# Two gates on weight splits: none beside a power on GpSimd, and few while ScalarE and VectorE have a backlog

## The chip, the core and the metric

The program runs on one core of a Trainium2 chip. The metric is the time of one execution in microseconds (us) of device time. Three runs of the kernel before gave 1283.79, 1284.68 and 1285.19 us, a median of 1284.68 us. A profiled execution of its own is the source of all rows below. TensorE is written PE in the rows (PEld is its weight load), VectorE DVE, ScalarE ACT, GpSimd POOL and SyncE SP.

## What is computed

Two blocks of two layers each on 256 tokens of width 1024, all in float32. The first block has a short convolution mixer, a SwiGLU feed-forward layer, a windowed attention with sinks (16 query heads, 4 key heads), and a second SwiGLU layer:

```
x = x + short_conv_mixer(rmsnorm(x)) ; x = x + swiglu_ffn(rmsnorm(x))
x = x + swa_sink_attention(rmsnorm(x)) ; x = x + swiglu_ffn(rmsnorm(x))
```

The second block has a mixed attention (8 windowed heads with rotary positions, 8 neighbourhood heads with a position bias), a squared-ReLU layer, a bidirectional Mamba-2 mixer (eight groups of four heads), and a squared-ReLU layer, each followed by a layer norm:

```
x = layer_norm(ALPHA * x + mix(x)) ; x = layer_norm(ALPHA * x + squared_relu_mlp(x))
```

In the first attention the queries and keys are normalised per head, and a softmax over 128 or 256 keys and one sink gives the weights. In the Mamba-2 mixer each group's result y is normalised: its squares are summed, the sum plus a small number is raised to the power -0.5, and y is multiplied by that.

## The kernel before

**Weights.** Every weight matrix is cut into units of 128 x 2048 numbers (201 units). A unit comes by one 1 MB transfer into one of three raw buffers. Since the fast matmul reads rounded numbers, a unit is split into two tiles, hi and lo, in four parts of 128 x 512: ScalarE casts hi<-raw, VectorE subtracts lo<-raw,hi (`split_part`). Each product of two such pairs takes three matmuls (hi hi, hi lo, lo hi). So there are 804 casts and 804 subtractions, 769 of them on VectorE and 35 on GpSimd, which `beside` puts there in the Mamba-2 mixer. Five buffers of split units exist.

**Order.** The order of all instructions is fixed while the program is written, by a planner: `Clock` keeps a modelled time for each engine, for each written tile and for PSUM banks, and each recorded instruction moves it. A main thread writes the big matmuls one after the other, and between groups of three it calls `step`, which first calls `Units.fill` and then `Side.run`. `fill` writes splits ahead of their use; `Side.run` advances side tasks (softmax of a pair of heads, transposes, norms), each of which names the tiles that it needs and is taken when the planner thinks that they are ready. Every engine then works through its own instructions strictly in that order.

**How far ahead.** `fill` counts the parts that are split and not yet in use. With fewer than 8 of them (two units) a split is "late" and is written at once, one in each step, whatever the engines have to do. With 8 or more it is written only if the planner sees both ScalarE and VectorE idle. `get` writes at once what a matmul needs and nobody has split.

**Places that matter here.** (1) `attn1`, the first attention: `tok_mm` for the values ends with a copy of the bank into the tile `vt` on ScalarE (`nc.scalar.copy(out=vt[:, t, :], in_=ps[:, 0:256])`); the side task `heads_out`, which multiplies softmax weights by `vt`, asks for the softmax weights and for the task that marks `vt` as written, not for the time at which it is written. The exponentials of the softmax stand on ScalarE too. (2) `group_out` in `ssm`, the Mamba-2 mixer: squares on ScalarE, `rstd` (one VectorE addition to a tile sm, then a power of 128 x 2 numbers on GpSimd), a scaling on ScalarE, four transposes on PE, and a second split of the result. (3) `w_half`, the output product of the mixer: `row_mm` reads four units of 12 matmuls for each half of the tokens, so it uses up a unit in the time of 12 matmuls of 512 columns. All operations are recorded by one helper, so nearly every row has the line L162; the tiles tell them apart (g and sm are pools of work tiles, bank is a PSUM bank, xt the transposed activations).

Of the kernel before, what the change touches and what calls it, by code (L numbers as in the profile page):

```python
# [29 lines left out]
def _free(ap):  # L30
    n = 1
    for s in ap.shape[1:]:
        n *= s
    return n


class Clock:
# [11 lines left out]
    def __init__(self):  # L49
        self.at = dict.fromkeys(self.LAG, 0.0)  # L50
        self.cold_until = 0.0
        self.port = 0.0
        self.written = {}
        self.read = {}
        self.floor = {}
        self.bank = {}
# [26 lines left out]
    def op(self, eng, cost, outs, ins, port=False):  # L83
        t = self.at[eng]
        if port:
            t = max(t, self.port)
        for a in ins:
            t = max(t, self.ready(a, eng))
        for a in outs:
            t = max(t, self.floor.get(a.tensor.name, 0.0))  # L90
        banks = [self.bank.setdefault(a.tensor.name, {}) for a in ins + outs if a.tensor.space == PSUM]
        for b in banks:
            t = max([t] + [end + 130.0 for e, end in b.items() if e != eng])
        if eng == "pe":
            if t - self.at[eng] > self.IDLE:
                self.cold_until = t + self.WARM
            if t < self.cold_until:
                cost *= 2.0
        end = t + cost
        self.at[eng] = end  # L100
        for b in banks:
            b[eng] = end
        if port:
            self.port = end
        for a in ins:
            n = a.tensor.name
            self.read[n] = max(self.read.get(n, 0.0), end)
        for a in outs:
            w = self.written.setdefault(a.tensor.name, {})
            for b in self.blocks(a):  # L110
                w[b] = (end, eng)


class Engine:
# [7 lines left out]
    def cost(self, op, out, ins, kw):  # L122
        n = _free(out)
        src = max(n, max((_free(a) for a in ins if a.tensor.name != out.tensor.name), default=0))
        if self.name == "pe":
            if op == "transpose":
                return 107.0
            if out.shape[0] == 64:
                return 2.5 + max(n, 128) / 1.2
            return 2.5 + (n / 2.4 if ins[0].dtype == F32R and n >= 256 else max(n, 128) / 0.6)  # L130
        from_psum = any(a.tensor.space == PSUM for a in ins)
        if self.name == "act":
            ptr = sum(not isinstance(kw.get(k, 0.0), (int, float)) for k in ("scale", "bias"))
            return (50 if from_psum else 95) + 0.833 * n + 93 * ptr + (90 if "accum_out" in kw else 0)
        if self.name == "dve":
            if op == "memset":
                return 60 + 0.26 * n
            if op == "reciprocal":
                return 65 + 6.3 * n
            n += 62 * any(hasattr(kw.get(k), "tensor") for k in ("scalar", "scalar1", "scalar2", "accum_out"))  # L140
            fast = op in ("tensor_copy", "tensor_scalar") and not from_psum and out.tensor.space != PSUM
            return 65 + (0.52 if fast else 1.04) * (src if op in ("tensor_reduce", "bn_stats") else n)
        return 300 + 165.0 * n if kw["op"] == ALU.pow else 125 + 2.15 * n

    def __getattr__(self, op):
        f = getattr(self.engine, op)

        def emit(*args, **kw):
            aps = [a for a in args if hasattr(a, "tensor")]
            outs = [kw[k] for k in ("out", "accum_out") if k in kw]  # L150
            ins = [v for k, v in kw.items() if k not in ("out", "accum_out") and hasattr(v, "tensor")]
            if not outs:
                outs, aps = aps[:1], aps[1:]
            ins = [a for a in aps + ins if a.tensor.name in self.clock.written]
            if self.name == "dma":
                n = outs[0].shape[0] * _free(outs[0]) * 4
                self.clock.op("dma", 60 + n / 359.0, [o for o in outs if o.tensor.space == bass.MemoryType.SB], ins)
            else:
                n_sb = sum(a.tensor.space != PSUM and _free(a) > 1 for a in ins)
                port = self.name == "pool" or self.name == "dve" and n_sb > 1  # L160
                self.clock.op(self.name, self.cost(op, outs[0], ins, kw), outs, ins, port)
            return f(*args, **kw)  # L162

        return emit
# [160 lines left out]
class Units:  # L325
# [2 lines left out]

    PARTS = 4
    AHEAD = 8  # L330

    def __init__(self, nc, clock, raw_pool, n_raw, w_pool, n_w):
        self.nc = nc
# [53 lines left out]
    def fill(self):  # L387

        at = self.clock.at
        while self.room():  # L390
            now = at["pe"] + 100.0
            late = self.parts - self.used * self.PARTS < self.AHEAD
            if self.clock.ready(self.raws[self.parts // self.PARTS], "act") > now:
                break
            if not late and (at["dve"] > now or at["act"] > now):
                break
            self.split_part()
            if late:
                break
# [1506 lines left out]
```

## Time and profile before

| what | value |
|---|---|
| median of three runs | 1284.68 us |
| profiled execution: its own time | 1285.68 us |
| span from first to last instruction | 1283.8 us |
| PE busy | 1255.0 us (98%) |
| VectorE, ScalarE, GpSimd busy | 951.9, 703.6, 82.4 us |
| mean granted TensorE clock | 0.993 |

A busy share is a share of the whole span; a matmul's end is modelled, so a busy PE can still have small gaps. The granted clock is 1.00 at 2.4 GHz and 0.50 at 1.2 GHz.

### The profile page before, as it was taken

The numbers are of one execution on the slowest core, as the hardware profiler recorded it, in microseconds if no ns is written. First come the engines' busy times: TensorE is split into PE (matmuls) and PEld (weight loads), VectorE is DVE, ScalarE is ACT, GpSimd is POOL, SyncE is SP. The second block draws the span as 40 slices with busy tenths as digits, with TensorE's granted clock in tenths as the row PEclk, the third lists the DMA queues.
The fourth block names the chain that finished last, engine by engine and source line by source line (L and its number), as shares of the span: only waits on it lengthen the run. The fifth ranks groups of instructions, "written<-read, shape, count | busy, mean of one in ns | idle before, by whom it ended". The sixth has DMA issues, their size and how long they took to land.

```text
span 1283.8 us, 18806 instructions
## 1 busy us (share of the span) xinstructions
PE 1255.0 (98%) x7092; PEld 1078.1 (84%) x7092; DVE 951.9 (74%) x1858; ACT 703.6 (55%) x1571; POOL 82.4 (6%) x69
## 2 busy tenths in 40 slices
PE   7999999999899999999999999999999989999997
PEld 6998888888678888888888888889989868888885
DVE  6776766677787666669788575689989878775665
ACT  5544555556665555556646464536777855554540
POOL 1000000002100000000000000002314130000000
PEclk9999999999899999999999999999999989999999
DMA  7753655546236555554447555454415144565530
GB/s 264 258 208 142 209 186 196 191 170 215 98 131 218 179 193 197 181 195 146 181 164 255 194 197 198 169 191 144 155 69 197 66 164 135 198 234 187 189 140 33
DMA packets 39436, 225.92 MB, mean 176 GB/s; under 512 B 5552, under 2 KB 7088, under 8 KB 13744
## 3 DMA queue, kind: packets, MB, share of 16 engines
q1 hardware_dynamic: 39344, 224.71, 49.5%
q8 instruction: 56, 0.92, 0.3%
q14 instruction: 36, 0.29, 0.1%
HBM read 223.51 MB, written 1.05 MB: 175 GB/s over the span
## 4 chain that ended last, share of the span: by engine, by line
PE 92%; DVE 4%; ACT 2%; DMA 1%; POOL 0%; issue 0%; SPq 0%; POOLq 0%; DVEq 0%; ACTq 0%
PE bank L162 92%; DVE g L162 3%; ACT g L162 1%; DVE lo L162 1%; DMA raw<-in_w_conv_in_dram 1%; POOL sm L162 0%; ACT hi L162 0%; DVE x L162 0%; SPq L162 0%; DVE sm L162 0%; ACT xt L162 0%; POOLq L1902 0%; DVE xt L162 0%; DVEq L1902 0%; ACT sm L162 0%
## 5 line engine op out<-in xcount | busy, mean ns | idle before, releaser
L162 PE MATMUL bank<-xt,hi 128*128 128x256 f32 (+1 forms) x1984 | 529.6, 340 | 0.2
L162 DVE TENSOR_TENSOR lo<-raw,hi 128x512 fp32r<-128x512 f32 x769 | 486.9, 689 | 45.7 <-ACT hi L162 38.4
L162 ACT CAST hi<-raw 128x512 fp32r<-128x512 f32 x804 | 444.6, 621 | 54.7 <-issue 31.8
L162 PE MATMUL bank<-xt,lo 128*128 128x256 f32 x1472 | 414.9, 282 | 0.0
L162 PEld LDWEIGHTS bank<-xt,hi 128*128 128x128 f32 x1984 | 342.2, 191 | 48.9 <-issue 1.6
L162 PE MATMUL bank<-hi,g 128*128 128x512 f32 x1184 | 381.0, 394 | 0.4 <-ACT g L162 0.2
L162 PEld LDWEIGHTS bank<-xt,lo 128*128 128x128 f32 x1472 | 280.0, 190 | 1.2
L162 PEld LDWEIGHTS bank<-hi,g 128*128 128x128 f32 x1184 | 223.0, 188 | 50.8 <-issue 2.3
L162 PE MATMUL bank<-lo,g 128*128 128x512 f32 x592 | 231.7, 391 | 1.5 <-DVE lo L162 1.5
L162 DVE TENSOR_TENSOR g<-bank,g 128x256 f32<-128x256 f32 (+5 forms) x210 | 95.1, 463 | 159.0 <-ACT g L162 153.0
L162 PE MATMUL bank<-hi,xt 128*128 128x512 f32 (+1 forms) x608 | 188.6, 380 | 0.0
L162 ACT COPY g<-bank 128x256 f32<-128x256 f32 (+2 forms) x163 | 66.6, 412 | 216.8 <-PE bank L162 216.6
L162 PEld LDWEIGHTS bank<-lo,g 128*128 128x128 f32 x592 | 111.7, 189 | 24.0 <-DVE lo L162 2.4
L162 PEld LDWEIGHTS bank<-hi,xt 128*128 128x128 f32 x608 | 111.4, 188 | 20.3 <-issue 0.3
L162 PE MATMUL bank<-lo,xt 128*128 128x512 f32 (+1 forms) x304 | 113.6, 374 | 0.0
L162 POOL TENSOR_TENSOR sm<-sm,nhalf 128x1 f32<-128x1 f32 (+3 forms) x30 | 33.4, 1113 | 1103.6 <-DVE sm L162 826.6
L162 DVE TENSOR_TENSOR g<-g,g 128x512 fp32r<-128x512 f32 (+4 forms) x99 | 63.6, 653 | 32.4 <-ACT g L162 31.6
L162 ACT CAST g<-g 128x512 fp32r<-128x512 f32 (+1 forms) x48 | 29.2, 611 | 79.5 <-DVE g L162 79.5
L162 PEld LDWEIGHTS bank<-lo,xt 128*128 128x128 f32 x304 | 57.4, 189 | 9.2 <-DVE lo L162 0.4
L162 PE MATMUL bank<-ident,g 128*128 128x128 f32 (+1 forms) x328 | 51.3, 289 | 12.5 <-DVE g L162 8.3
L162 PEld LDWEIGHTS bank<-ident,g 128*128 128x128 f32 x328 | 41.8, 149 | 23.5 <-DVE g L162 9.3
L162 PE MATMUL bank<-g,g 128*128 128x64 f32 (+6 forms) x428 | 54.4, 332 | 4.3 <-ACT g L162 4.3
(83 smaller groups left out, 721.8 us busy)
## 6 DMA issues: line engine op xcount, KB each, us to landing
raw<-in_w_mlp_dram SPq DMA_DIRECT2D x64, 1024.0 KB, 4.9
raw<-in_w_gate_up_dram SPq DMA_DIRECT2D x44, 1024.0 KB, 4.9
raw<-in_w_in_s_dram SPq DMA_DIRECT2D x24, 1024.0 KB, 4.9
raw<-in_w_down_dram SPq DMA_DIRECT2D x22, 1024.0 KB, 4.9
raw<-in_w_conv_in_dram SPq DMA_DIRECT2D x11, 1024.0 KB, 5.7
raw<-in_w_in_dram SPq DMA_DIRECT2D x8, 1024.0 KB, 4.9
raw<-in_w_out_s_dram SPq DMA_DIRECT2D x8, 1024.0 KB, 4.9
raw<-in_w_conv_out_dram SPq DMA_DIRECT2D x4, 1024.0 KB, 5.0
```

What stands on the lines that cost most here:

```text
L162: return f(*args, **kw)
```

## The change

The planner remembers when the last power on GpSimd ends (any GpSimd instruction with at most 8 numbers a partition), and `fill` has two new gates. A split is late if fewer than 4 parts are ahead, or if fewer than 8 are ahead and neither VectorE nor ScalarE is modelled to be busy for more than 1200 ns beyond now. And with at least 4 parts ahead none is written while the last power ends later than what VectorE has been given.

```diff
+        self.power = 0.0
...
+        if eng == "pool" and _free(outs[0]) <= 8:
+            self.power = end
...
+    SHORT = 1200.0
...
-            late = self.parts - self.used * self.PARTS < self.AHEAD
+            ahead = self.parts - self.used * self.PARTS
+
+            late = ahead < self.PARTS or ahead < self.AHEAD and max(at["dve"], at["act"]) < now + self.SHORT
             if self.clock.ready(self.raws[self.parts // self.PARTS], "act") > now:
                 break
+
+            if ahead >= self.PARTS and self.clock.power > at["dve"]:
+                break
             if not late and (at["dve"] > now or at["act"] > now):
                 break
```

No instruction is added or removed: casts, subtractions and matmuls are as many as before, and 35 subtractions stay on GpSimd. What moves is the order, since a split that comes elsewhere moves the planner's clocks and with them the side tasks. Up to the first attention the orders are nearly alike; in both attentions and in the Mamba-2 mixer they differ in many places.

ScalarE in the first attention, from the exponentials of the second token half to the copy into `vt` (tile g_2838) of the first half. Before:

```order
L162 ACTIVATE g_3264<-bank 128x512
L162 ACTIVATE g_3212,sm<-g_3212,sm 128x256 x2
L162 ACTIVATE g_3213,sm<-g_3213,sm 128x256 x2
L162 ACTIVATE sm<-sm 128x4
L162 ACTIVATE g_3235,sm<-g_3235,sm 128x256 x2
L162 ACTIVATE g_3236,sm<-g_3236,sm 128x256 x2
L162 ACTIVATE sm<-sm 128x4
L162 CAST hi<-raw 128x512 x4
L162 COPY g_2838<-bank 128x256
```

Now (g_3172, g_3173, g_3188 and g_3189 are the same softmax tiles; their exponentials stand just ahead of this piece):

```order
L165 ACTIVATE sm<-sm 128x4
L165 CAST hi<-raw 128x512
L165 ACTIVATE g_3228<-bank 128x512
L165 CAST hi<-raw 128x512
L165 ACTIVATE g_3267<-bank 128x512
L165 CAST hi<-raw 128x512
L165 COPY g_3285<-bank 128x512
L165 CAST hi<-raw 128x512 x2
L165 COPY g_3309<-bank 128x512
L165 CAST hi<-raw 128x512
L165 COPY g_2838<-bank 128x256
```

The eight exponentials and four casts stood right before the copy; now the squares of two query chunks and the copies of the transposed softmax tiles (g_3285, g_3309) lie between, with one cast at the end. On PE the transposes of those softmax tiles stand among the 24 value matmuls of the first half, where they came after the multiplication by `vt` before.

VectorE at the start of `w_half`, around the addition (TENSOR_SCALAR sm<-sm) that feeds the power of group 6. Before (g_10364 and g_10198 are convolution results of group 7):

```order
L162 SCALAR_TENSOR_TENSOR g_10364<-bank,wc,g_10364 128x255 x4
L162 SCALAR_TENSOR_TENSOR g_10364<-bank,wc,g_10364 128x254 x4
L162 SCALAR_TENSOR_TENSOR g_10198<-g_10351,g_10198 128x512
L162 TENSOR_TENSOR lo<-raw,hi 128x512 x2
L162 TENSOR_SCALAR sm<-sm 128x2
L162 TENSOR_TENSOR lo<-raw,hi 128x512 x4
L162 SCALAR_TENSOR_TENSOR g_10364<-g_10436,g_10364 128x512
L162 TENSOR_TENSOR lo<-raw,hi 128x512 x3
L162 SCALAR_TENSOR_TENSOR g_10527<-bank,sm,g_10526 128x256 x2
```

Now (g_10363 and g_10231 are those results):

```order
L165 TENSOR_TENSOR lo<-raw,hi 128x512
L165 SCALAR_TENSOR_TENSOR g_10231<-g_10352,g_10231 128x512
L165 SCALAR_TENSOR_TENSOR g_10363<-bank,wc,g_10363 128x255 x4
L165 SCALAR_TENSOR_TENSOR g_10363<-bank,wc,g_10363 128x254 x4
L165 TENSOR_SCALAR sm<-sm 128x2
L165 TENSOR_TENSOR lo<-raw,hi 128x512 x3
L165 SCALAR_TENSOR_TENSOR g_10363<-g_10434,g_10363 128x512
L165 TENSOR_TENSOR lo<-raw,hi 128x512 x4
L165 SCALAR_TENSOR_TENSOR g_10502<-bank,sm,g_10501 128x256 x2
```

Behind the addition stand three subtractions, a gate product and four more subtractions, where there were four, the product and three. The two subtractions that stood just ahead of it are gone from there.

ScalarE at the same place, from the squares of group 6 to its scaling (g_10187 before, g_10196 now), which waits for the power. Before:

```order
L162 ACTIVATE g_10408,sm<-g_10187 128x256 x2
L162 CAST hi<-raw 128x512 x4
L162 ACTIVATE g_10436<-g_10364 128x512
L162 CAST hi<-raw 128x512 x3
L162 ACTIVATE g_10187<-g_10187,sm 128x256 x2
```

Now:

```order
L165 ACTIVATE g_10360,sm<-g_10196 128x256 x2
L165 CAST hi<-raw 128x512 x3
L165 ACTIVATE g_10434<-g_10363 128x512
L165 CAST hi<-raw 128x512
L165 ACTIVATE g_10196<-g_10196,sm 128x256 x2
L165 CAST hi<-raw 128x512 x3
```

Seven casts stood between the squares and the scaling; now there are four, and the next three come behind the scaling.

## Rows read from the trace of the kernel before

**Rows 1.** The page: busy time of the engines, share of the span, instructions

```profile
PE 1255.0 (98%) x7092; PEld 1078.1 (84%) x7092; DVE 951.9 (74%) x1858; ACT 703.6 (55%) x1571; POOL 82.4 (6%) x69
```

**Rows 2.** Waits of PE: who waited for whom: total us, times, longest us

```profile
PE bank L162 <- DVE g L162: 9.1, 3, 8.3
PE bank L162 <- ACT g L162: 8.5, 3, 4.3
PE bank L162 <- DVE lo L162: 1.5, 2, 1.3
```

**Rows 3.** Windows: length, then each engine's busy us (instructions), granted clock, DMA

```profile
331.90:336.50 4.60, 0.33 (x3) 0.13 (x2) 4.07 (x16) 4.55 (x16) 1.64 (x1) 0.76 0.00 0
336.50:341.20 4.70, 4.69 (x17) 3.08 (x18) 2.96 (x6) 1.92 (x4) 0.00 (x0) 0.50 0.30 82
...
1040.90:1049.20 8.30, 2.80 (x10) 1.34 (x8) 7.16 (x14) 2.76 (x7) 5.29 (x1) 0.91 0.69 255
1049.20:1054.50 5.30, 5.29 (x14) 4.19 (x15) 2.16 (x4) 1.20 (x3) 0.00 (x0) 0.50 0.53 195
```

**Rows 4.** Timeline of PE, first attention: start, length, what, idle before, releaser

```profile
331.95 0.28 PE L162 MATMUL bank<-hi,xt 128*128 128x256 f32 x1
336.51 1.98 PE L162 MATMUL bank<-g,g 128*64 128x512 f32 x4 [4.27 <-ACT g L162]
...
346.00 0.28 PE L162 MATMUL bank<-hi,xt 128*128 128x256 f32 x1
```

**Rows 5.** Timeline of ACT there: four casts, and both copies into vt

```profile
334.03 2.16 ACT L162 CAST hi<-raw 128x512 fp32r<-128x512 f32 x4
336.10 0.36 ACT L162 COPY g<-bank 128x256 f32<-128x256 f32 x1
...
346.51 0.34 ACT L162 COPY g<-bank 128x256 f32<-128x256 f32 x1
```

**Rows 6.** Timeline of PE around the start of w_half

```profile
1033.05 0.40 PE L162 MATMUL bank<-xt,hi 128*128 128x256 f32 x2
...
1033.41 0.40 PE L162 MATMUL bank<-hi,g 128*128 128x512 f32 x1
...
1040.69 0.61 PE L162 MATMUL bank<-hi,g 128*128 128x512 f32 x2
1042.63 0.50 PE L162 MATMUL bank<-lo,g 128*128 128x512 f32 x1 [1.32 <-DVE lo L162]
...
1049.21 1.30 PE L162 MATMUL bank<-ident,g 128*128 128x128 f32 x4 [3.98 <-ACT g L162]
```

**Rows 7.** Timeline of POOL: four of the eight powers of the Mamba-2 mixer

```profile
945.34 1.08 POOL L162 TENSOR_TENSOR sm<-sm,nhalf 128x2 f32<-128x2 f32 x1 [6.14 <-DVE sm L162]
...
1023.48 0.70 POOL L162 TENSOR_TENSOR sm<-sm,nhalf 128x2 f32<-128x2 f32 x1 [8.48 <-DVE sm L162]
...
1043.33 5.29 POOL L162 TENSOR_TENSOR sm<-sm,nhalf 128x2 f32<-128x2 f32 x1 [5.36 <-DVE sm L162]
1075.52 1.07 POOL L162 TENSOR_TENSOR sm<-sm,nhalf 128x2 f32<-128x2 f32 x1 [26.90 <-DVE sm L162]
```

**Rows 8.** Timeline of DVE around the power at 1043.33

```profile
1038.17 3.20 DVE L162 SCALAR_TENSOR_TENSOR g<-bank,wc,g 128x255 f32<-128x255 f32 x8
...
1043.17 2.49 DVE L162 TENSOR_TENSOR lo<-raw,hi 128x512 fp32r<-128x512 f32 x4
...
1046.17 1.89 DVE L162 TENSOR_TENSOR lo<-raw,hi 128x512 fp32r<-128x512 f32 x3
```

**Rows 9.** Timeline of DVE beside the powers at 945.34 and 1075.52

```profile
945.17 1.89 DVE L162 TENSOR_TENSOR lo<-raw,hi 128x512 fp32r<-128x512 f32 x3
...
1075.35 1.89 DVE L162 TENSOR_TENSOR lo<-raw,hi 128x512 fp32r<-128x512 f32 x3
```

**Rows 10.** Timeline of ACT at the start of w_half, and the scaling after the power

```profile
1033.62 1.02 ACT L162 ACTIVATE g<-bank,wc 128x256 f32<-128x256 f32 x2 [2.80 <-PE bank L162]
...
1048.65 0.91 ACT L162 ACTIVATE g<-g,sm 128x256 f32<-128x256 f32 x2 [5.06 <-POOL sm L162]
```

## The prediction

> **What bounds the kernel now.** I read the busy times first: TensorE is busy for 1255.0 us of a span of 1283.8 us [rows 1], so the kernel is its stream of matmuls, and only time that TensorE loses can be won. The waits of TensorE come next: 9.1, 8.5 and 1.5 us [rows 2]. One of these, 8.3 us, is the start of the program, which the change leaves as it is. What is left is 10.8 us, and two places hold nearly all of it; the windows and timelines show them.
>
> The first is in the first attention. The value matmuls of the first token half end at about 332.2, and TensorE then idles for 4.27 us until 336.51 [rows 4]. It waits for the copy of these values into `vt`, 0.36 us on ScalarE. That copy starts only at 336.10, behind the exponentials and four casts of 2.16 us together [rows 5]. After the pause the granted clock is 0.50, 1.2 GHz: from 336.50 to 341.20 TensorE is busy for 4.69 us at half speed [rows 3], which costs about 2.35 us more. Together 6.6 us.
>
> The second is in the Mamba-2 mixer, at the start of `w_half`. TensorE waits 1.32 us (1.5 with the small one after it [rows 2]) for a `lo` tile, and then 3.98 us for a scaling on ScalarE [rows 6]. The scaling had waited 5.06 us for a power [rows 10]. That power took 5.29 us, where others of its size took 0.70 to 1.08 [rows 7]. It ended 0.56 us after the last of a row of subtractions and products on VectorE that started at 1043.17 and ended at 1048.06 [rows 7, 8]. Then 5.29 us of matmuls ran at a clock of 0.50 [rows 3], which costs 2.65. Together 1.5 + 4.0 + 2.65 = 8.2 us (rounded).
>
> **The change part by part.** Nothing is added or removed on any engine, so busy time is the same, and what counts is where TensorE waits in the new order.
>
> *The copy into `vt`.* In the new order the eight exponentials stand well ahead, and right before the copy stand one softmax copy and one cast. On TensorE the transposes which that softmax copy reads are followed by 15 value matmuls of 256 columns. Three such matmuls start within 1033.41 - 1033.05 = 0.36 us [rows 6], so 15 take 1.8 us, and two ScalarE instructions of 0.5 to 0.6 us [rows 5] fit in. So the copy comes without a queue. `heads_out` is still placed right behind the value matmuls, so TensorE waits for the bare copy: the second copy started 0.51 us after the last value matmul had started and took 0.34 [rows 4, 5], 0.85 us, of which one matmul's 0.12 us is no wait. I take 0.8 us, and no lower clock, since the two drops of this trace stand behind pauses of 4 us. Saved: 6.6 - 0.8 = 5.8 us. Bounds: 0 if something of the old length is in front of it again, 6.6 if the copy is hidden.
>
> *The power.* I count from S, the first matmul of `w_half` (1033.41 before). Before, VectorE did the last eight convolution steps from S + 4.8 [rows 8], since group 6's result came late; in the new order the matmuls that give this result stand 48 matmuls of 256 columns ahead of S instead of 12, so that group's arithmetic on VectorE lies mostly ahead of S, and the convolution steps wait only for the ScalarE instruction that starts them, S + 0.2 to S + 1.2 [rows 10]. They take 3.2 us [rows 8]: S + 4.4. The addition follows, and the power starts at about S + 4.6. With 0.70 to 1.08 us [rows 7] it ends by S + 5.7, the scaling of 0.91 us [rows 10] by S + 6.7. Its transposes stand behind 33 matmuls; before, 32 of these started within 1040.69 - 1033.41 = 7.28 us [rows 6], so they come at S + 7.5. Slack 0.8 us: no wait.
>
> But the gate does not keep the splits away here. Three subtractions, a product and four more subtractions stand right behind the addition, because fewer than four parts are ahead in `w_half` and the power gate doesn't hold then. If the power is held as before, VectorE still runs dry sooner: only one cast is left before the scaling, so after five instructions of 0.62 us each (2.49 / 4 [rows 8]) VectorE has to wait, at S + 7.7. The power then ends 0.56 later at S + 8.3, the scaling at S + 9.2, and TensorE waits 1.7 us. How often is a power held? Three powers have three or more subtractions beside them: at 945.34 and 1075.52 they took 1.08 and 1.07 [rows 7, 9], at 1043.33 it took 5.29. One in three; I take the short one.
>
> The Trainium skill, "SBUF — State Buffer", section "Who interferes with whom", says that a VectorE instruction with two SBUF inputs and a GpSimd instruction that reads SBUF shut each other out, whoever starts first. The row at 1043.33 agrees, those at 945.34 and 1075.52 agree for the first subtraction only. By the rule taken to its end the new order would block this power as well, which is the first rival below.
>
> *The late `lo`.* TensorE waited because the convolution steps stood in front of the twelfth subtraction for `w_half`. Now the three subtractions behind the addition include the twelfth: S + 4.6 + 3 x 0.62 = S + 6.5, and it is read by the 34th matmul, after S + 7.5. So the 1.5 us go too, with 1.0 us to spare. Saved at this place: 8.2 us; between 3.9 (held power, and the low clock again: 8.2 - 1.7 - 2.65) and 8.2.
>
> *New waits.* The attentions and the eight groups are laid out anew, and the planner still doesn't see every wait: side tasks that ask for a task and not for a time, copies that land behind four exponentials of 0.5 us. The trace can't show them. Beside the two places TensorE lost 10.8 - 4.3 - 4.0 - 1.5 = 1.0 us in the whole kernel [rows 2]. The bounds for new ones are 0 and 6.6 us, one more of the kind of `vt`. I take 3: the two attentions and the groups were nearly free of waits before, and a new layout is more likely to have some.
>
> **Sum.** 5.8 + 8.2 - 3 = 11.0 us. The profiled execution took 1285.68 us (its span 1283.8 and 1.9 around it), so it would take 1274.7; it lies 1.0 us above the median of the runs, 1284.68, so the median would be 1273.7. I say 1274. The forecast's own range is 1270 to 1277.5: 14.0 us saved without new waits, about 7 with the full 6.6.
>
> **Rivals.**
>
> *The power is held again* (the change doesn't do what it says at the place that matters). For it: the three subtractions right behind the addition. Against it: two of three such powers were not held. The saving is 5.8 + 3.9 - 3 = 6.7 us: 1278. The same time results if the copy waits as before and the power is free (8.2 - 3 = 5.2: 1279.5).
>
> *The waits move.* Two new waits of the kind of `vt`, each 4.27 us and 2.35 us of low clock: 14.0 - 13.2 = 0.8 us saved, 1284, no change. For it: in the second half of the first attention the copies of `heads_out` now stand behind eight exponentials (4 us), where before four of them stood in front. Against it: 18 matmuls of 512 columns, 4.1 us by the rate above, cover most of that.
>
> *Splits come too late* (slower). Both gates let TensorE come closer to the split parts, four instead of eight ahead in a backlog. A subtraction that lands behind a convolution step then costs what it cost at 1042.63, about 1.5 us with its follower [rows 2], once for each of the 32 units of the Mamba-2 mixer at worst. Slower starts where such waits eat the 14.0 us and 2.6 more: 11 of them; with 16 it is 14.0 - 24 = -10, 1295 us. For it: when `w_half` starts, nine parts of its weights are split in the new order, eleven before. Against it: from the start to 290 us and from 400 to 575 the two orders are nearly alike, and nine parts are three quarters of what the first 36 matmuls use.
>
> **How the numbers follow.** Forecast (both waits gone): 0.50. Held power, or one of the two places only: 0.25. Moved waits, no change: 0.12. Late splits, slower: 0.13. Runs of this kernel can tell 0.2%, 2.6 us, from no change. So faster 0.75, the same 0.12, slower 0.13. The range of eight in ten starts at 1268, a little below all savings without a new wait (1270.7), and ends at 1285, so that it holds the no-change case; the late splits are left out above it.
>
> **What would show it.** Right: no idle of TensorE over 1 us behind the value matmuls of the first attention, no stretch at a clock of 0.50 between the start and the end, and the power of group 6 at about 1 us. The first rival: a power of 3 to 4 us beside subtractions, and TensorE waiting for ScalarE behind 33 matmuls of `w_half`. The second: new waits of PE for ACT g of 3 us or more in the attentions. The third: the total of PE waiting for DVE lo at 15 us or more. The forecast as a whole is wrong if busy time of TensorE at full clock changes by more than 2 us, since no instruction was added.

## The result, and the profile after

The changed kernel took 1299.07 us (median of four runs, 1298.61 to 1301.63), the kernel before 1284.24 (four runs, 1283.63 to 1285.19). The ratio is 1.0119, with a 95% interval of 1.0106 to 1.0132. It is slower by 15 us, where 1274 had been forecast. Its profiled execution took 1298.61 us with a span of 1296.8, 13.0 more than before. Rows of the changed kernel have the line L165 where those of before have L162.

The page of the changed kernel, busy time of the engines, is the counterpart of [rows 1]:

```profile
PE 1257.8 (97%) x7092; PEld 1081.8 (83%) x7092; DVE 943.1 (73%) x1858; ACT 704.1 (54%) x1571; POOL 75.5 (6%) x69
```

No instruction was added. PE's busy time grew by 2.8 us, which is matmuls at a lower clock (below); the other 10 of the 13 us are idle time of PE. The waits of PE after (who waited for whom, total us, times, longest us), against [rows 2]:

```profile
PE bank L165 <- DVE lo L165: 10.9, 10, 4.2
PE bank L165 <- DVE g L165: 9.5, 2, 9.2
PE bank L165 <- ACT hi L165: 7.2, 5, 2.5
PE bank L165 <- ACT g L165: 1.9, 3, 1.0
PE bank L165 <- POOL lo L165: 0.7, 2, 0.4
```

The wait for DVE g is still the start of the program, 0.9 us longer than before. The waits for ACT g, which the forecast wanted to remove, fell from 8.5 to 1.9 us. But PE now waits for the split weights themselves, hi and lo: 10.9 + 7.2 + 0.7 = 18.8 us in 17 waits, where there were 1.5 in two.

The longest of these waits is in the first attention. The timeline of PE there (start, length, what, idle before and its releaser):

```profile
315.78 0.39 PE L165 MATMUL bank<-hi,xt 128*128 128x512 f32 x1
316.37 0.50 PE L165 MATMUL bank<-hi,xt 128*128 128x512 f32 x1 [0.20 <-ACT hi L165]
321.08 0.65 PE L165 MATMUL bank<-lo,xt 128*128 128x512 f32 x1 [4.21 <-DVE lo L165]
```

The timeline of VectorE ahead of it shows what stood in front of that `lo`:

```profile
303.28 0.68 DVE L165 TENSOR_TENSOR lo<-raw,hi 128x512 fp32r<-128x512 f32 x1
305.50 0.69 DVE L165 TENSOR_TENSOR g<-bank,sm 128x512 f32<-128x512 f32 x1 [1.54 <-POOL sm L165]
...
309.82 0.69 DVE L165 TENSOR_TENSOR lo<-raw,hi 128x512 fp32r<-128x512 f32 x1 [1.28 <-ACT hi L165]
...
315.84 0.69 DVE L165 TENSOR_REDUCE sm<-g 128x8 f32<-128x512 f32 x1 [2.52 <-ACT g L165]
...
318.55 0.69 DVE L165 TENSOR_TENSOR g<-bank,sm 128x512 f32<-128x512 f32 x1 [0.63 <-POOL sm L165]
...
319.55 0.88 DVE L165 TENSOR_SCALAR g<-g,sm 128x128 f32<-128x128 f32 x4
320.34 3.09 DVE L165 TENSOR_TENSOR lo<-raw,hi 128x512 fp32r<-128x512 f32 x5
```

Between 303.28 and 320.34 VectorE wrote one part, though it idled five times (four of them, 1.54, 1.28, 2.52 and 0.63 us, are in these rows). Then five subtractions came at once, behind two rounds of softmax and a head norm. How many parts were written shows in the windows of VectorE, counting only its `lo` instructions (length, busy us and number, clock, DMA). Before:

```profile
280.00:300.00 20.00, 8.02 (x13) 1.00 0.55 190
300.00:320.00 20.00, 7.10 (x11) 1.00 0.57 206
```

After:

```profile
280.00:300.00 20.00, 6.12 (x10) 1.00 0.53 185
300.00:320.00 20.00, 3.35 (x5) 1.00 0.45 159
```

Five against eleven: in the same 20 us TensorE ate what had been split ahead and then stood still.

Behind the pauses the clock fell. The windows of the three stretches at half clock (compare [rows 3]; a stretch behind the last weight matmul, which both kernels have, is left out):

```profile
321.30:324.70 3.40, 3.40 (x16) 2.77 (x15) 2.13 (x4) 1.27 (x2) 0.00 (x0) 0.50 0.37 96
355.40:362.20 6.80, 5.33 (x22) 4.27 (x24) 4.18 (x10) 1.48 (x3) 0.00 (x0) 0.50 0.46 153
1041.50:1048.30 6.80, 6.64 (x31) 6.64 (x32) 5.19 (x10) 2.71 (x6) 0.00 (x0) 0.50 0.52 166
```

15.37 us of busy time at half speed cost 7.7 us, where the 4.69 + 5.29 us of before cost 5.0 [rows 3]. The difference, 2.7 us, is nearly all of the 2.8 us of busy time.

At the two places of the forecast the waits did shrink. The copy into `vt` is now bare; the row answers to [rows 4]:

```profile
337.98 0.28 PE L165 MATMUL bank<-hi,xt 128*128 128x256 f32 x1
338.78 1.08 PE L165 MATMUL bank<-g,g 128*64 128x512 f32 x4 [0.52 <-ACT g L165]
```

And at the start of `w_half` the power of group 6 was held again, but shorter, as the first rival had worked out. First POOL, then the subtractions of VectorE beside it, then PE (compare [rows 6, 7, 8]):

```profile
1060.25 3.48 POOL L165 TENSOR_TENSOR sm<-sm,nhalf 128x2 f32<-128x2 f32 x1 [0.26 <-DVE sm L165]
```

```profile
1060.08 1.89 DVE L165 TENSOR_TENSOR lo<-raw,hi 128x512 fp32r<-128x512 f32 x3
```

```profile
1062.91 0.39 PE L165 MATMUL bank<-hi,g 128*128 128x512 f32 x1
1064.33 0.94 PE L165 MATMUL bank<-ident,g 128*128 128x128 f32 x4 [1.03 <-ACT g L165]
```

The account: at the two places 4.27 - 0.52 + 2.35 = 6.1 us and 1.5 + 3.98 - 1.03 + 2.65 = 7.1 us came in. The split waits and the clock behind them took 18.8 + 7.7 = 26.5. That makes 13.3 us longer; the span says 13.0. By place the 26.5 us are 14.4 in the first attention (10.0 of waits, the rest clock), 1.7 in the second and 10.4 in the Mamba-2 mixer (7.1 of waits, 5.4 of them for casts, and clock). The close agreement is in part luck: the first attention lost 10.6 us (table below), where these terms give 14.4 - 6.1 = 8.3, and the stretch ahead of that attention was 1.3 us shorter in this execution than in that of before.

### The profile page after: what moved, and what is told of

It is laid out like the page before. It is cut to its first block, busy times and chain, and to the rows that moved or that the text cites. A ratio compares the mean times of both kernels' runs of the same rounds, so it can differ in the third digit from the quotient of the medians.

```text
span 1296.8 us, 18810 instructions
## 1 busy us (share of the span) xinstructions
PE 1257.8 (97%) x7092; PEld 1081.8 (83%) x7092; DVE 943.1 (73%) x1858; ACT 704.1 (54%) x1571; POOL 75.5 (6%) x69
## 4 chain that ended last, share of the span: by engine, by line
PE 62%; DVE 4%; ACT 2%; issue 1%; POOL 1%; POOLq 0%; DVEq 0%; ACTq 0%
PE bank L165 62%; DVE g L165 2%; ACT g L165 2%; DVE lo L165 1%; POOL sm L165 0%; ACT hi L165 0%; DVE sm L165 0%; DVE x L165 0%; POOL lo L165 0%; POOLq L1911 0%; DVE xt L165 0%; DVEq L1911 0%; DVE dt L165 0%; ACT sm L165 0%; POOLq L165 0%
## 5 line engine op out<-in xcount | busy, mean ns | idle before, releaser
L165 PE MATMUL bank<-xt,hi 128*128 128x256 f32 (+1 forms) x1984 | 530.4, 341 | 5.5 <-ACT hi L165 5.4
L165 DVE TENSOR_TENSOR lo<-raw,hi 128x512 fp32r<-128x512 f32 x769 | 485.5, 685 | 56.3 <-ACT hi L165 47.8
L165 ACT CAST hi<-raw 128x512 fp32r<-128x512 f32 x804 | 446.6, 624 | 65.9 <-issue 28.8
L165 PE MATMUL bank<-xt,lo 128*128 128x256 f32 x1472 | 416.5, 283 | 3.4 <-DVE lo L165 2.7
L165 PEld LDWEIGHTS bank<-xt,hi 128*128 128x128 f32 x1984 | 342.5, 191 | 53.1 <-ACT hi L165 6.0
L165 PE MATMUL bank<-hi,g 128*128 128x512 f32 x1184 | 378.2, 392 | 1.6 <-ACT hi L165 1.6
L165 PEld LDWEIGHTS bank<-xt,lo 128*128 128x128 f32 x1472 | 280.5, 191 | 6.6 <-DVE lo L165 4.3
L165 PEld LDWEIGHTS bank<-hi,g 128*128 128x128 f32 x1184 | 222.4, 188 | 51.7 <-issue 2.6
L165 PE MATMUL bank<-lo,g 128*128 128x512 f32 x592 | 231.3, 391 | 4.0 <-DVE lo L165 4.0
L165 DVE TENSOR_TENSOR g<-bank,g 128x256 f32<-128x256 f32 (+5 forms) x210 | 95.1, 463 | 158.1 <-ACT g L165 151.6
L165 PE MATMUL bank<-hi,xt 128*128 128x512 f32 (+1 forms) x608 | 188.9, 380 | 0.2 <-ACT hi L165 0.2
L165 ACT COPY g<-bank 128x256 f32<-128x256 f32 (+2 forms) x163 | 66.8, 415 | 214.8 <-PE bank L165 214.6
L165 PEld LDWEIGHTS bank<-lo,g 128*128 128x128 f32 x592 | 111.4, 188 | 26.8 <-DVE lo L165 5.1
L165 PEld LDWEIGHTS bank<-hi,xt 128*128 128x128 f32 x608 | 111.7, 188 | 20.6 <-ACT hi L165 0.6
L165 PE MATMUL bank<-lo,xt 128*128 128x512 f32 (+1 forms) x304 | 113.9, 375 | 4.3 <-DVE lo L165 4.2
L165 POOL TENSOR_TENSOR sm<-sm,nhalf 128x1 f32<-128x1 f32 (+3 forms) x30 | 30.7, 1024 | 1096.2 <-DVE sm L165 807.1
L165 DVE TENSOR_TENSOR g<-g,g 128x512 fp32r<-128x512 f32 (+4 forms) x99 | 59.2, 608 | 32.8 <-ACT g L165 32.0
L165 ACT CAST g<-g 128x512 fp32r<-128x512 f32 (+1 forms) x48 | 29.2, 611 | 77.3 <-DVE g L165 77.3
L165 PEld LDWEIGHTS bank<-lo,xt 128*128 128x128 f32 x304 | 57.4, 189 | 14.0 <-DVE lo L165 5.0
L165 DVE SCALAR_TENSOR_TENSOR g<-bank,wc,g 128x255 f32<-128x255 f32 (+1 forms) x128 | 51.4, 473 | 15.0 <-ACT g L165 14.8
L165 PE MATMUL bank<-ident,g 128*128 128x128 f32 (+1 forms) x328 | 50.6, 290 | 10.3 <-DVE g L165 9.2
L165 PEld LDWEIGHTS bank<-ident,g 128*128 128x128 f32 x328 | 42.1, 150 | 18.7 <-DVE g L165 9.2
```

## The experiments

**The theories.** A: the backlog gate lets the lead of split parts shrink, and TensorE waits for hi and lo. B: the power gate is what holds the splits back. C: any new layout of the side tasks brings new waits, whatever the lead. D, about the kernel before: the wait for the copy into `vt` is worth its 6.6 us.

**The measure of the lead.** It is counted in the program as it is written: when a unit is first asked for, how many parts from that unit on are split. Four means that only its own parts are there and nothing of the next one. Before it is 8.2 on average over the units of the first attention, and 8 at the least; after it is 4.9, and 4 for six units in a row.

**The measure by stage.** All kernels read the weights in the same order, so the same weight matmul marks the same place in each. The table gives the time between two such places minus that of before: first attention (299 to 391 us of before), second (580 to 680), Mamba-2 mixer (873 to 1110). What is missing to the total is mostly the stretch ahead of the first attention, which differs by up to 1.7 us from that of before. Each such number comes from one trace, and where TensorE pauses the clock alone can move it by 1.5 us (last section). The ratios are to runs of before on the same chip as the kernel, with medians of 1284.23 to 1284.68 us. The edits of e1, e2, e3 and e7 are to the changed kernel, those of e4 and e5 to the kernel before.

| kernel | median us | ratio to before, 95% | mean lead: 1st att., 2nd att., Mamba input | us against before: 1st, 2nd, Mamba | PE waits for hi, lo us |
|---|---|---|---|---|---|
| before | 1284.24 | 1 | 8.2, 8.7, 9.0 | 0, 0, 0 | 1.5 |
| after | 1299.07 | 1.0106 to 1.0132 | 4.9, 8.1, 6.5 | +10.6, +1.3, +3.5 | 18.8 |
| e1 power gate | 1273.74 | 0.9905 to 0.9930 | 7.6, 8.7, 8.8 | -2.9, 0, -7.9 | 0 |
| e2 backlog gate | 1292.34 | 1.0051 to 1.0078 | 5.2, 8.1, 6.5 | +8.4, +1.3, +1.4 | 12.4 |
| e3 both, from six | 1295.07 | 1.0068 to 1.0094 | 6.5, 7.9, 7.3 | +5.7, +4.4, +1.5 | 9.1 |
| e4 vt's time | 1279.79 | 0.9954 to 0.9980 | 8.2, 8.7, 9.0 | -3.8, 0, -0.7 | 1.5 |
| e5 lead four | 1313.86 | 1.0214 to 1.0245 | 4.4, 5.5, 5.5 | +13.5, +9.1, +6.1 | 26.6 |
| e6 power gate, vt | 1272.91 | 0.9898 to 0.9925 | 7.6, 8.7, 8.8 | -4.2, 0, -7.9 | 0 |
| e7 no backlog gate in 1st | 1286.55 | 1.0007 to 1.0025 | 7.6, 8.1, 6.5 | -2.6, +1.3, +5.1 | 7.8 |
| e8 as e6, twelve | 1283.61 | 0.9979 to 0.9998 | 11.1, 11.9, 12.2 | -5.2, +0.4, +3.5 | 0 |
| e9 as e6, six | 1287.05 | 1.0008 to 1.0028 | 6.2, 7.2, 7.2 | +2.2, +5.1, -2.7 | 9.0 |
| e10 as e6, ten | 1272.76 | 0.9888 to 0.9918 | 9.9, 10.2, 10.7 | -5.1, +1.2, -6.9 | 0 |

**e1, the power gate alone.**

```diff
-            late = ahead < self.PARTS or ahead < self.AHEAD and max(at["dve"], at["act"]) < now + self.SHORT
+            late = ahead < self.AHEAD
```

> Only the power gate; a split is late with fewer than 8 parts ahead, as before. Theory A (the backlog gate cuts the lead, so TensorE waits for hi and lo): lead at first use in the first attention is 7.6 parts on average (before 8.2, after 4.9), so waits of TensorE for hi and lo stay under 4 us, and the time is at or below that of before, 1276 to 1286 us. Theory B (the power gate is what holds splits back): splits wait as in the changed kernel, 1292 to 1300 us. Theory C (any new layout of the side tasks brings new waits, whatever the lead): slower than before by 5 us or more, with waits behind g tiles as often as behind hi or lo.

1273.74 us (1272.93 to 1274.39), 0.8% faster than before. There is no wait for hi or lo. In the Mamba-2 mixer 7.9 us came in: the power of group 6 has only two subtractions behind its addition, and then products that read a bank. POOL and DVE of e1:

```profile
1042.89 1.67 POOL L165 TENSOR_TENSOR sm<-sm,nhalf 128x2 f32<-128x2 f32 x1 [7.76 <-DVE sm L165]
```

```profile
1042.72 1.28 DVE L165 TENSOR_TENSOR lo<-raw,hi 128x512 fp32r<-128x512 f32 x2
1043.92 1.28 DVE L165 SCALAR_TENSOR_TENSOR x<-x,bank 128x512 f32<-128x512 f32 x2
```

TensorE has no wait at the start of `w_half`, and no half clock between 15 us and the last weight matmul. Theory A's forecast of a time at or below that of before holds (the time is 2 us below its range), B and C do not: this is another layout too, and its longest new wait is one of 1.1 us.

**e2, the backlog gate alone.**

```diff
-            if ahead >= self.PARTS and self.clock.power > at["dve"]:
-                break
```

> Only the backlog gate; no gate on powers. Theory A: lead in the first attention 5.2 parts (after 4.9), in the Mamba-2 mixer as in the changed kernel, so nearly all of the loss is there: 1293 to 1301 us, 14 us or more of waits of TensorE for hi and lo. Theory B: as before, 1281 to 1287 us. Theory C: anywhere above 1289 us, not tied to hi and lo.

1292.34 us: more than half of the loss is here. The waits of PE:

```profile
PE bank L165 <- DVE lo L165: 7.1, 7, 2.8
PE bank L165 <- ACT hi L165: 4.9, 2, 2.5
```

With 0.4 us for POOL lo they make 12.4, a little under the 14 that A expected, as the time is 0.7 us under its range, and the first attention loses 8.4 us. Theory B is out. The time lies in C's range too, but the waits are for hi and lo. The changed kernel is 6.7 us slower by the medians. The two profiled executions differ by 2.5 only, since that of e2, 1296.12 us, is the slowest of its six (1289.40 to 1296.12), and that of the changed kernel the fastest of its four. So the power gate, which makes the kernel faster by itself, does not do so beside the backlog gate.

**e3, both gates from six parts on.**

```diff
-            late = ahead < self.PARTS or ...
+            late = ahead < self.FLOOR or ...
-            if ahead >= self.PARTS and self.clock.power > at["dve"]:
+            if ahead >= self.FLOOR and self.clock.power > at["dve"]:
+    FLOOR = 6
```

> Both gates, but with 6 parts in place of 4 as the number from which they act. Theory A: lead in the first attention 6.5 parts, between the 4.9 of the changed kernel and the 8.2 of before, and the loss falls with it: 1284 to 1294 us, waits for hi and lo 3 to 10 us. Theory C: no order in the number of parts, as slow as the changed kernel or slower, 1297 us or more, or at random.

1295.07 us, 1 us outside A's range and too fast for the 1297 of C. By stages: the first attention loses 5.7 us, between 10.6 and 0, as A wants. The second loses 4.4, more than the changed kernel, which the lead does not explain (7.9 on average and 4 at the least, against 8.1 and 2); in the trace 1.39 us of it is a wait for lo and 0.80 one for g, in the output product of that attention, where the changed kernel has no wait. So the total does not follow the number of parts, though the first attention does.

**e4, vt's time.**

```diff
-        yield Need(*pT[0], *pT[1], banks=1)
+        yield Need(*pT[0], *pT[1], *vals, banks=1)
...
-                hs + vdone[:t + 1],
+                hs + vdone[:t + 1], [vt[:, j, :] for j in range(t + 1)],
```

> The kernel before, no gates; heads_out of the first attention also names the written tiles of vt, so that it is taken when the planner thinks the copy is done. Theory D (the wait for the copy into vt and the low clock after it cost before 6.6 us, and no other work of TensorE is missing there): 1277 to 1281 us, no half-clock stretch in the first attention. Rival: the second half's value matmuls now stand right behind the first half's and the wait only moves behind them (both copies stand behind the same exponentials and casts on ScalarE): a wait of 2 to 4 us remains and the time is 1281 to 1285 us.

1279.79 us. The window over that place shows TensorE busy throughout at full clock:

```profile
329.00:345.00 16.00, 16.00 (x111) 11.38 (x111) 15.22 (x62) 13.86 (x51) 1.64 (x1) 1.00 0.19 67
```

So the 6.6 us are gone there. At the end of the stage 3.8 of them are left: two new waits for VectorE's g tiles come later in it, 1.4 us together; the other 1.4 is in no wait of the list. Theory D's range holds, and part of the rival too. This edit is independent of the gates.

**e5, a lead of four without gates**, on the kernel before.

```diff
-    AHEAD = 8
+    AHEAD = 4
```

> The kernel before without either gate, but a split is late only with fewer than 4 parts ahead (AHEAD 4 in place of 8). This is the cut of the lead alone, everywhere. Lead at first use: first attention 4.4 parts (before 8.2, after 4.9), second 5.5 (8.7, 8.1), Mamba-2 mixer 5.5 (9.0, 6.5). Theory A (a short lead makes the splits late): slower than the changed kernel, 1299 to 1320 us, with waits of TensorE for hi and lo above the 18.8 us of the changed kernel. Rival (it is not the lead but the test of the backlog that writes splits at bad places): no slower than before by more than 5 us, under 1289 us.

1313.86 us. No power gate, no test of the backlog, only the smaller lead: the loss of the changed kernel and more, by the same waits.

```profile
PE bank L162 <- DVE lo L162: 19.4, 13, 4.2
PE bank L162 <- DVE g L162: 9.5, 3, 9.0
PE bank L162 <- ACT hi L162: 6.4, 6, 2.3
```

**e6, the power gate with vt's time**: e1 and e4 together.

> The power gate alone together with the time of vt in heads_out. The power gate alone left one wait of TensorE of 3.23 us for the copy into vt. Theory D (this wait is all that is there): 1269 to 1272 us. Rival (the second half's value matmuls and later transposes take the wait over, as about 2.5 of 6.6 us came back behind the place when vt's time was named without a gate): 1272 to 1274.5 us.

1272.91 us (1272.03 to 1275.10). It beats both kernels of the case. Against e1 the difference cannot be told from none: of the 3.23 us that e1 lost behind the copy into `vt`, 0.35 were left, and two waits for VectorE of 0.96 and 1.28 us came later in the stage, as the rival said.

**e7, no backlog gate in the first attention**, on the changed kernel.

```diff
+        units.SHORT = 1e9
         nsink = negated(a["sinks"], 16)
...
-        return attention("wo", oT, finish, done)
+        norms = attention("wo", oT, finish, done)
+        units.SHORT = 1200.0
+        return norms
```

> The changed kernel with the backlog gate off inside the first attention (any part short of 8 is late there), on elsewhere; the power gate stays everywhere. Lead in the first attention 7.6 parts, as with the power gate alone; elsewhere as in the changed kernel. Theory A: the first attention gives back the 10.6 us that it lost and the 1 to 2 us that the power gate alone won there: 1285 to 1289 us, no wait for hi or lo between 300 and 390 us. Rival (the stages after it are laid out by what the first attention leaves, and the loss comes back there): 1294 us or more.

1286.55 us, in A's range: 12.5 us come back by a gate switched off in 90 us of the program. PE's waits from 299 to 400 us, after and in e7 (those for hi, lo and the copy into `vt`, which is ACT g):

```profile
PE bank L165 <- DVE lo L165: 8.2, 4, 4.2
PE bank L165 <- ACT hi L165: 1.8, 2, 1.6
PE bank L165 <- ACT g L165: 0.5, 1, 0.5
```

```profile
PE bank L165 <- ACT g L165: 3.2, 1, 3.2
```

What is left against e1, 12.8 us, is the backlog gate behind the first attention, nearly all of it in the Mamba-2 mixer: -7.9 there in e1, +5.1 here. Of the 5.1 us about 1.5 are clock alone: the changed kernel has the same order there and lost 3.5.

**e8, e9, e10: twelve, six and ten parts**, each e6 with another AHEAD.

```diff
-    AHEAD = 8
+    AHEAD = 12
```

> Power gate and the time of vt, and 12 parts in place of 8 below which a split is late. Lead in the first attention 11.1 parts, Mamba-2 mixer 12.2. Theory A taken further (more lead, fewer waits): no wait for hi or lo is left with 8 already, so nothing to win: within 3 us of the kernel with 8. Rival (more splits in front of the side work delay it, as four casts in front of the copy into vt did): 4 us or more slower than with 8, with waits behind g tiles.

> Power gate and the time of vt, and 6 parts in place of 8 below which a split is late. Lead at first use: first attention 6.2 parts, second 7.2, Mamba-2 mixer 7.2. Theory A with the dose of the runs so far (first attention: 6.5 parts lost 5.7 us against before, 8 with the same two edits won 4.2; second attention 4 to 9 lost at 5.5 to 7.9 parts): 1284 to 1294 us, with waits for hi and lo of 3 us or more. Rival (the loss came from the test of the backlog and not from the number of parts; a plain lead of six covers the side work): 1271 to 1278 us.

> Power gate and the time of vt, and 10 parts in place of 8. Theory A says that 8 is enough for hi and lo, and the side work pays for more: between the 1272.9 us with 8 and the 1283.6 us with 12, 1273 to 1281 us, with waits behind g tiles. Rival (12 was an accident of one place in the Mamba-2 mixer): 1269 to 1273 us.

Six: 1287.05, eight: 1272.91, ten: 1272.76, twelve: 1283.61 us. With six TensorE waits for splits again (9.0 us). With twelve it waits for none, as with eight and ten, but the splits now stand in front of the side work: PE's waits for DVE g are 17.2 us, 9.7 of them the start (11.4 and 8.5 with eight), and in the output product a group's result comes late. PE, ACT and DVE of e8:

```profile
1070.09 0.39 PE L165 MATMUL bank<-hi,g 128*128 128x512 f32 x1
1073.86 1.30 PE L165 MATMUL bank<-ident,g 128*128 128x128 f32 x4 [3.38 <-ACT g L165]
```

```profile
1062.31 3.79 ACT L165 CAST hi<-raw 128x512 fp32r<-128x512 f32 x7
1071.24 0.42 ACT L165 ACTIVATE g<-g 128x256 f32<-128x256 f32 x1 [5.14 <-DVE g L165]
```

```profile
1065.85 4.29 DVE L165 TENSOR_TENSOR lo<-raw,hi 128x512 fp32r<-128x512 f32 x7
```

So in e8 the rival held, in e9 theory A. e10 lies 0.2 us below A's range and inside that of its rival, which called twelve an accident of one place: ten is as good as eight. The trace of e8 shows three such places, not one: waits of 2.18, 2.96 and 3.38 us in the Mamba-2 mixer, where e6 and e10 have none above 1.21. That the loss grows with the number of parts is not shown; ten does not have it, and twelve does.

## Why the prediction was wrong

**Nothing is added or removed: right.** Busy time of PE changed by 2.8 us, all of it by the clock.

**The copy into `vt`: right.** From the start of the last value matmul to the product 0.85 us were forecast; it is 0.80 (337.98 to 338.78), 0.52 of it idle, without low clock. 6.1 us came in, 5.8 was said.

**The power: the rival had the mechanism, and that the saving came near the term is luck.** I took the short one, 8.2 us saved, with "one in three" held. It was held for 3.48 us, and TensorE waited 1.03 us for the scaling behind it; S + 4.6 to S + 8.3, so 3.7, and 1.7 had been worked out for that case. The low clock that I added to that case did not come, so 7.1 us were won, where the term said 8.2 and the rival 3.9.

**New waits: this step failed.** It said 3 us, between 0 and 6.6, and argued from the kernel before: "the two attentions and the groups were nearly free of waits before". Measured: 26.5 us, four times the upper bound. Before was free of them because each unit of the attentions and the mixer had at least six parts split when it was first asked for, eight in the first attention, and that is what the change takes away. A bound taken from the waits of a kernel whose cover is being removed bounds nothing; the bound had to come from the cover.

**The third rival named the mechanism and one of the two places.** It put 16 waits of 1.5 us into the Mamba-2 mixer, 1295 us; measured were 17 waits of 1.1 us and the clock, 1299, but nine of these waits in the mixer (7.1 us), most of that for casts, and six in the first attention (10.0 us). That the total came so near is in part luck. Its own sign, 15 us of waits for DVE lo, did not come either: these were 10.9, and 18.8 only with hi and GpSimd's lo. I gave it 0.13 because "from the start to 290 us and from 400 to 575 the two orders are nearly alike". The stretch in between, 290 to 400, is the first attention, where the largest loss is (10.6 us; e7 gives it back). And I tested the lead only at `w_half`, nine parts against eleven, where it still was enough. Counting it at each unit of the first attention in the new order, 10, 6, 4, 5, 4, 4, 4, 4, 4, 4 against 10 and nine times 8, would have shown the fall without a run, though not its price.

**Why the lead falls there.** The planner must find both VectorE and ScalarE with less than 1200 ns of work beyond now, at the moment of a step. While a softmax is queued on one of them the gate says no, although in the trace both engines idle between its pieces. What is not written then is written when fewer than four parts are left, and so behind the softmax. That the shrinking lead is the cause is shown: e2 and e5 bring the loss, e1 and e7 take it away, and over the kernels without e4's edit the first attention loses more the smaller its lead is (7.6: -2.9 and -2.6, 6.5: +5.7, 5.2: +8.4, 4.9: +10.6, 4.4: +13.5; the gain at 7.6 is the shorter wait for `vt`). The wait for `vt` is in these numbers, 4.27 us before, 3.23 at a lead of 7.6, 4.21 at 6.5, 2.85 at 5.2 and about 0.5 at 4.9 and 4.4, so without it the loss would rise more steeply still. Counted in the planner, 61 of its steps in the first attention found four to seven parts ahead: 47 were refused by the backlog test, every time with VectorE beyond the 1200 ns and 11 times with ScalarE too, 9 by the power gate, and 5 wrote a part. That it is the softmax which fills VectorE there is read from the order and the trace, not tried by itself.

**What stays open.** Why the second attention lost more with six parts than with four. And why e2 and the changed kernel, with the same mean lead on the input units of the Mamba-2 mixer, differ by 2 us there: TensorE waits 5.9 and 8.1 us in it, and 1.0 us of that difference is the wait behind the held power, which took 1.07 us in e2; the rest are waits for splits.

## What to carry to other kernels

Work that is done ahead and costs nothing now is the cover of a stage; before a gate thins it out, count what is left of it at each use, in every stage, and above all where the engines that do the work are busy with something else. A rule that postpones work "while there is a backlog" postpones it in just those stages where it then has to queue. When two gates come in one change, try each alone: here one alone was 10.5 us faster than before, and the other, beside it, cost 25.

## What the runs showed of the hardware

**When a power gets in.** I had taken the hold of a power as a matter of chance, one in three. It is not: kernels with the same piece of order repeat it to 0.01 us (5.29, 5.28 and 5.29 us in before, e4 and e3; 4.08 in e1 and e6; 3.48 in after and e7). In the twelve traces 20 powers of the mixer's groups have a row of subtractions behind their addition, the first of them just started. Ten took 1.07 to 1.19 us, ten took 1.67 to 5.29. In the first ten the subtractions ran hard on the heels of their casts: the second one started 0.13 to 0.53 us after its own cast had ended. In the other ten the casts were further ahead: 0.82 us at the least, up to 3.89. Two from before; first ScalarE's casts for the subtractions that start at 945.17 [rows 9], where cast and subtraction keep step and the power took 1.08 us:

```profile
944.14 1.67 ACT L162 CAST hi<-raw 128x512 fp32r<-128x512 f32 x3
```

and the casts for the first four subtractions at 1043.17 [rows 8], long done, where it took 5.29:

```profile
1038.76 2.17 ACT L162 CAST hi<-raw 128x512 fp32r<-128x512 f32 x4
```

The Trainium skill, "SBUF — State Buffer", section "Who interferes with whom", has VectorE instructions with two SBUF inputs and GpSimd instructions that read SBUF shut each other out. The held ten agree with that to the end, the others only for the first subtraction. It may be that a VectorE instruction which has only just become ready lets the power in; the rows show no gap for it, since in both groups the second subtraction starts 0.07 to 0.09 us before the first one ends, and no run took that apart.

**The same pause, another clock.** In e1 and e7 TensorE waits 3.23 us behind the same value matmuls for the same copy. In e7 the clock then is 0.50, in e1 it stays 1.00. Windows of the 3.4 us behind the pause, e1 and e7:

```profile
334.20:337.60 3.40, 3.40 (x26) 2.42 (x26) 3.33 (x10) 2.54 (x6) 0.00 (x0) 1.00 0.00 0
```

```profile
333.70:337.10 3.40, 3.40 (x16) 2.97 (x15) 3.36 (x10) 1.92 (x4) 0.00 (x0) 0.50 0.00 0
```

The changed kernel and e7 show the same with nothing else changed: behind the first attention, from 404 us of the changed kernel on, their rows are the same in the same order on all four engines. The same wait for a cast in the Mamba-2 mixer, the changed kernel first, then e7:

```profile
970.68 0.51 PE L165 MATMUL bank<-xt,hi 128*128 128x256 f32 x2 [2.48 <-ACT hi L165]
```

```profile
957.35 0.51 PE L165 MATMUL bank<-xt,hi 128*128 128x256 f32 x2 [2.46 <-ACT hi L165]
```

And the stretches behind it, in the same order:

```profile
971.70:975.00 3.30, 3.30 (x31) 3.30 (x29) 3.27 (x7) 3.22 (x7) 0.00 (x0) 1.00 0.44 112
```

```profile
958.40:961.70 3.30, 3.30 (x18) 3.30 (x17) 2.90 (x6) 2.80 (x7) 0.00 (x0) 0.50 0.37 117
```

Over the whole mixer e7 took 1.5 us more. So a pause of 2.5 to 3.2 us costs between nothing and 1.7 us of clock here, and two kernels with such pauses that differ by less than that cannot be ranked by one profile.
